# Router logits from rows that are not normalised yet, and a combine with sums and norms fused tile by tile

## The chip, the core and the metric

The kernel is one program on 1 core of one Trainium2 chip. Its time is device microseconds from start to end of one execution; the inputs lie in the chip's memory. The engines are TensorE (PE, matmuls and transposes), VectorE (DVE), ScalarE (ACT), GpSimd (POOL) and SyncE (SP), which issues most of the loads. Each engine runs its own instructions in the order in which the program lists them and waits for the others by semaphores.

## The reference

A first block (four mixers and a dense feed-forward) makes 512 rows of 1024 columns from `x`. Then 16 meta rows are put ahead of them and two layers follow. A layer is a mixer and a mixture of 32 experts, each with a layer norm behind it:

```python
for i in range(2):
    mixed = rglru_mixer(h, ...) if i == 0 else shortconv_mixer(h, ...)
    h = layer_norm(ALPHA * h + mixed, ln_g[i, 0], ln_b[i, 0])
    ffn = hierarchical_moe(h, ...)     # router on h, best group, best two of its eight experts
    h = layer_norm(ALPHA * h + ffn, ln_g[i, 1], ln_b[i, 1])
return h[:, 16:]

# layer_norm
mu = mean(x); var = mean((x - mu) ** 2)
y = (x - mu) * rsqrt(var + 1e-5) * g + b
# router
glog = h @ w_group + b_group           # 4 columns
elog = h @ w_expert + b_expert         # 32 columns
# lru mixer ends in (scan * gelu) @ w_out; short convolution:
zc = causal_conv(cg * v); mixed = (bg * zc) @ w_out
```

Only the last two meta rows matter to what is returned, since the short convolution of layer 1 looks back by two rows.

## The kernel before

The rows are kept as four tiles `xt` of 128 rows, and a fifth, `hm`, of the two meta rows, which lives until the short convolution. Products that need full precision are made in three passes of a split: a rounded half (`zh`, `hhi`, `sh_0h`, made by ACT) and the rest (`zl`, `hlo`, `sh_0l`, made by DVE).

**From the mixer to the router** (`mix_ln`, twice). `token_mm` multiplies the mixer's result by `w_out`, tile by tile and in two halves of 512 columns, into `pz`; the last tile of rows comes last. With `steps` set, `sum_` (L1830) adds `pz` to the row tile as soon as a half is there. `ln_sums` (L1622) squares on ACT, small operations on DVE make the mean (`lnm`) and the scale (`lnrr`), `ln_norm` (L1629) normalises on ACT. `Moe.xpose` transposes the normalised tile on PE (`prt`), DVE and ACT copy it (`rht`, L2061), `Moe.route` multiplies it by the router's weights `wr` (36 columns) and adds the bias row `brt` by one more product (`plg`). `ln_gain` (L1638) applies the norm's gain and bias, on DVE and, for a part of the columns of all but the last tile, on POOL. `Moe.fold` has multiplied the gain into `wr` and the bias into `brt` (PE: `pbr<-wr,par`), so the router works on rows without gain. Behind the last tile `Moe.logits` copies all logits (L2078), and the router's choice begins with `gm` (L2114).

**The experts** (`moe`). 32 experts' weights are streamed by SP through buffers `sr`; PE multiplies sorted rows by them. Each row's two results are kept in memory.

**The combine** (end of `moe`). For each tile the two results `cy` are read back, scaled by the gates `gt`, added to the rows, and normalised. The table `COMBINE` sets in which order the steps of the tiles are written: S sums, N norm, G gain, T transposes for the next mixer; M is a form for the meta rows in layer 0 that uses ACT and POOL. `GPC` says how many columns of a gain are DVE's, the rest are POOL's. In layer 0 the meta rows come first, and T of tiles 2 and 3 is left to the short convolution (`e.left`).

**The short convolution** (`shortconv`) multiplies the transposed rows in two halves of columns `HV`, of 258 and 256, the first with the two meta columns ahead.

Of the kernel before, what the change touches and what calls it, by code (L numbers as in the profile page):

```python
# [8 lines left out]
F32 = mybir.dt.float32  # L9
# [8 lines left out]
P = 128  # L18
S = 512
# [26 lines left out]
ORDER[NP // 2:NP // 2] = range(NST, NST + MORE)  # L46
NB = (NP + MORE + 1) // 2 * 2
CT = 32
GPC = ((640, 448, 640, 384, 448), (832, 832, 512, 320))
COMBINE = ("M4 S0 S1 N0 N1 S2 S4 N4 G0 G1 G4 T0 T1 T4 S3 N2 G2 N3 G3", "S0 S1 N0 S2 N1 S3 N2 G0 G1 N3 G2 G3")  # L50
MOE_W = ("moe_w_gate_2", "moe_w_up_2", "moe_w_down_2")
EPS = 1e-6
LN_EPS = 1e-5
# [1442 lines left out]
def token_mm(e, nk, xx, done, tiles, before_tail=None, tail=8, steps=False):  # L1496

    left = deque()
    st = e.st
    for h in range(2):
        pz = [e.bank(f"pz{t}") for t in range(len(tiles))]

        def part(w, k, i):
            tk = tiles[i]
            e.mm3(pz[i][:tk.stop - tk.start], (xx[0][k][:, tk], xx[1][k][:, tk]), (w[0], w[1]), k == 0, k == nk - 1)

        k = 0
# [8 lines left out]
        if h == 1:  # L1520
            if before_tail:
                before_tail()
            ww = [st.get() for _ in range(tail // 2)]
            for i in range(len(tiles)):
                for j in range(tail):
                    part([x[:, j % 2, :] for x in ww[j // 2]], nk - tail + j, i)
                if steps:
                    new = done(i, 1, pz[i])
                    last = list(left)[-1:]
                    with e.tc.manual_schedule(engines=VA):  # L1530
                        for g in [new] + last + [new] + last:
                            next(g)
                        if len(left) > 1:
                            next(left.popleft(), None)
                    left.append(new)
                    continue
                if len(left) >= 2:
                    left.popleft()()
                left.append(done(i, 1, pz[i]))
    return left  # L1540
# [271 lines left out]
def mix_ln(e, sp, zz, tiles, hs, mo):  # L1812


    e.st.limit = e.mark2 if mo.l else e.mark
    g = e.brow(sp, "ln_g_2", D, off=(mo.l * 2) * D, tag="lng0")
    b = e.brow(sp, "ln_b_2", D, off=(mo.l * 2) * D, tag="lnb0")
    sums = {}
    mo.fold()

    def done(i, h, p_):
        if h:
            return steps(i, p_)
        sum_(i, h, p_)

    def sum_(i, h, p_):
        n = tiles[i].stop - tiles[i].start
        c = slice(h * 512, h * 512 + 512)
        s_ = sums[i, h] = sp.tile([P, 1], F32, name=f"sum{i}{h}")[:n]
        e.V.scalar_tensor_tensor(hs[i][:, c], hs[i][:, c], ALPHA, p_[:n], op0=OP.mult, op1=OP.add, accum_out=s_)  # L1830

    def steps(i, p_):
        sum_(i, 1, p_)
        n = tiles[i].stop - tiles[i].start
        nm, ss = ln_sums(e, sp, hs[i], n, [sums[i, 0], sums[i, 1]], sp.tile([P, D], BF, name="lnj")[:n])
        yield
        ln_norm(e, sp, hs[i], n, nm, ss)
        yield
        ht = mo.xpose(sp, hs[i], n)
        yield  # L1840
        t = i - (len(tiles) - NT)
        t = NT if t < 0 else t
        ln_gain(e, hs[i], n, g, b, 0 if i == len(tiles) - 1 else 448)
        mo.keep(t, hs[i], n)
        yield
        mo.route(ht, t, n)

# [47 lines left out]
def shortconv(e):  # L1895
    tc, I, st, sch = e.tc, e.I, e.st, e.sch
    V, A, G, Q = e.V, e.A, e.G, e.Q
    xt, bank, pc = e.xt, e.bank, e.pc
    TH = 258
    HV = (slice(0, TH), slice(TH, TK))  # L1900
    e.mo = Moe(e, 1, None)
    zp = tc.tile_pool(name="sz", bufs=1, reuse_waits="tile")
    zpool = zp.__enter__()
# [2 lines left out]
    sp = sp_.__enter__()  # L1906

    def put(kind, cg, pr, hv, p_):
        if kind == 0:
            A.copy(cg[:, hv], p_)  # L1910
        else:
            e.mul(pr[:, hv], cg[:, hv], p_)
# [9 lines left out]
    for j in range(0, KT, 2):  # L1922
# [40 lines left out]
class Moe:  # L1963
# [76 lines left out]

        self.e.G.dma_start(self.dh[t * P:t * P + n, :], h)

    def fold(self):

        e = self.e
        pg, pb = [e.pc((n, 2 * D) if self.l else n, 0, KT) for n in ("ln_g_2", "ln_b_2")]
        pt = e.bank("pbr")[0:1, :36]
        for k in range(KT):
            e.mm(pt, pb[:, k:k + 1], self.wr[:, k, :], k == 0, k == KT - 1)
        e.add(self.br, self.br, pt)  # L2050
        e.mul(self.wr, self.wr, pg.unsqueeze(2).to_broadcast([P, KT, 36]))
# [12 lines left out]
    def route(self, ht, t, n):  # L2064

        e = self.e
        if self.pl is None:
            self.pl = e.bank("plg"), (e.bank("plg") if self.nt > NT else None)
        pl = self.pl[0][:, t * 36:(t + 1) * 36] if t < NT else self.pl[1][:n, :36]
        for k in range(KT):  # L2070
            e.mm(pl, ht[:, k, :n], self.wr[:, k, :], k == 0, False)
        e.mm(pl, self.one[:, :n], self.br[0:1, :], False, True)
        if t == NT:
            e.A.copy(self.lg[:n, t, :], pl)

    def logits(self):

        self.done = self.e.A.copy(self.lg[:, :NT, :].rearrange("p t c -> p (t c)"), self.pl[0][:, :NT * 36])  # L2078

    def run(self):  # L2080
        moe(self.e, self)
# [3 lines left out]
def moe(e, mo):  # L2085
# [406 lines left out]
        e.act3 = tc.tile_pool(name="act3", bufs=1, side="right", reuse_waits="tile")  # L2492
        e.open_act(e.act3.__enter__())
    with tc.tile_pool(name=f"cb{l}", bufs=1, reuse_waits="tile") as sp:
        order = [NT, 0, 1, 2, 3] if l == 0 else range(NT)
        ys = {}
        with tc.manual_schedule(engines={mybir.EngineType.SP}):
            for t in order:
                if l == 0 and t == NT - 1:
                    st.stop()  # L2500
                    st.prefetch()
                n = rows_[t][1]
                ys[t] = sp.tile([P, 2, D], F32, name="cy", bufs=4)
                Q.dma_start(ys[t][:n], dy[2 * t * P:2 * (t * P + n), :].rearrange("(t k) c -> t k c", k=2))
        def sums(h, n, t):
            y_ = ys[t][:n]
            stt(h, y_[:, 0, :], gt[:n, t, 0:1], h, OP.mult, OP.add)
            sm = sp.tile([P, 1], F32, name="csum", bufs=4)[:n]
            V.scalar_tensor_tensor(h, y_[:, 1, :], gt[:n, t, 1:2], h, op0=OP.mult, op1=OP.add, accum_out=sm)  # L2509
            return ln_sums(e, sp, h, n, [sm], y_[:, 0, :])  # L2510

        def scaled(h, n, t):

            y_ = ys[t][:n]
            for k in range(2):
                A.activation(y_[:, k, :], y_[:, k, :], AF.Copy, scale=gt[:n, t, k:k + 1])
                G.tensor_tensor(h, h, y_[:, k, :], op=OP.add)
            yield
            sm = sp.tile([P, 1], F32, name="msum")[:n]
            A.activation(y_[:, 0, :], h, AF.Identity, accum_out=sm)  # L2520
            yield ln_sums(e, sp, h, n, [sm], y_[:, 0, :], "m")

        def step(c, t):
            h, n = rows_[t]
            if c == "M":
                ms[t] = scaled(h, n, t)
                next(ms[t])
            elif c == "S":
                ms[t] = next(ms[t]) if t == NT else sums(h, n, t)
            elif c == "N":  # L2530
                ln_norm(e, sp, h, n, *ms[t], "m" if t == NT else "")
            elif c == "G":
                ln_gain(e, h, n, g, b, GPC[l][t])
                if l == 1:
                    Q.dma_start(e.out[0, t * P:(t + 1) * P, :], h)
            else:
                e.tile_to_fm(h, 2 + t * P if t < NT else 0, n)

        ms = {}
        with tc.manual_schedule(engines={mybir.EngineType.DVE, mybir.EngineType.Activation, mybir.EngineType.Pool}):  # L2540
            t = order[0]
# [40 lines left out]
```

## Time and profile before

| | us |
|---|---|
| median of 3 runs | 2554.92 (2554.54 to 2555.36) |
| the profiled execution | 2554.61 |
| its span | 2552.8 |
| PE busy | 2300.2 (90%) |
| DVE busy | 944.4 (37%) |
| ACT busy | 666.8 (26%) |
| POOL busy | 226.5 (9%) |

The span is divided into the first block, the lru mixer (to about 1260), the experts of layer 0 (to about 1757), the combine and the short convolution (to about 2005), the experts of layer 1 and the last combine. Over most of the expert layers the DMA moves 412 to 419 GB/s. The granted clock of PE was 0.964 in the mean; between stretches it takes the levels 0.5 (1.2 GHz) and 1.0 (2.4 GHz).

### The profile page before, as it was taken

The numbers are of one execution on the slowest core, as the hardware profiler recorded it, in microseconds if no ns is written. First come the engines' busy times: TensorE is split into PE (matmuls) and PEld (weight loads), VectorE is DVE, ScalarE is ACT, GpSimd is POOL, SyncE is SP. The second block draws the span as 40 slices with busy tenths as digits, with TensorE's granted clock in tenths as the row PEclk, the third lists the DMA queues.
The fourth block names the chain that finished last, engine by engine and source line by source line (L and its number), as shares of the span: only waits on it lengthen the run. The fifth ranks groups of instructions, "written<-read, shape, count | busy, mean of one in ns | idle before, by whom it ended". The sixth has DMA issues, their size and how long they took to land. (4 is left out here: it accounts for less than half of the span.)

```text
span 2552.8 us, 37528 instructions
## 1 busy us (share of the span) xinstructions
PE 2300.2 (90%) x15343; PEld 1470.3 (58%) x15343; DVE 944.4 (37%) x2162; ACT 666.8 (26%) x1058; POOL 226.5 (9%) x264
## 2 busy tenths in 40 slices
PE   7998999999999999999799899884899798899881
PEld 6886777877888888887632233221798532233220
DVE  4348868765533332565620000003644610000003
ACT  4335432123422322375300000013322210000012
POOL 0023120000100000100200000001200210000002
PEclk9999999999999999999799999997899799999996
DMA  4221221025133242224589999998225599999993
GB/s 142 91 80 43 87 70 63 23 79 187 53 106 92 90 140 91 80 82 147 221 342 418 419 415 416 412 415 313 61 87 227 224 399 418 419 413 414 415 405 122
DMA packets 176434, 556.87 MB, mean 218 GB/s; under 512 B 22248, under 2 KB 104934, under 8 KB 127106
## 3 DMA queue, kind: packets, MB, share of 16 engines
q1 hardware_dynamic: 154308, 523.29, 53.0%
q0 software_dynamic: 12768, 25.31, 2.7%
q10 hardware_dynamic: 9184, 5.84, 0.8%
q8 instruction: 122, 2.00, 0.3%
q14 instruction: 52, 0.43, 0.1%
HBM read 548.02 MB, written 25.21 MB: 225 GB/s over the span
## 5 line engine op out<-in xcount | busy, mean ns | idle before, releaser
L300 PE MATMUL peg<-sr,ext 128*32 128x512 f32 (+1 forms) x4064 | 527.6, 599 | 70.9 <-DMA sr<-in_moe_w_gate_dram 38.7
L300 PEld LDWEIGHTS peg<-sr,ext 128*32 128x32 f32 (+1 forms) x4064 | 142.4, 111 | 410.8 <-issue 276.7
L300 PE MATMUL pey<-sr,eh 128*32 128x512 f32 x1984 | 303.3, 597 | 14.1 <-DMA sr<-in_moe_w_down_dram 11.8
L300 PEld LDWEIGHTS pey<-sr,eh 128*32 128x32 f32 x1984 | 82.0, 110 | 193.5 <-issue 148.6
L227 DVE TENSOR_TENSOR sh_0l<-sr,sh_0h 128x1024 fp32r<-128x1024 f32 x84 | 103.5, 1232 | 163.4 <-ACT sh_0h L225 162.8
L285 DVE TENSOR_TENSOR eh<-eh,peg 128x512 f32<-128x512 f32 x34 | 23.4, 688 | 367.4 <-PE peg L300 367.4
L2321 ACT COPY eys<-pey 128x512 f32<-128x512 f32 x68 | 39.9, 586 | 428.9 <-PE pey L300 428.4
L225 ACT CAST sh_0h<-sr 128x1024 fp32r<-128x1024 f32 x84 | 88.1, 1049 | 238.4 <-PE pf L300 53.2
L2264 DVE COPY ext<-pex 128x512 f32<-128x512 f32 x32 | 22.0, 689 | 311.1 <-PE pex L319 311.1
L227 DVE TENSOR_TENSOR sh_1l<-sr,sh_1h 128x1024 fp32r<-128x1024 f32 (+1 forms) x65 | 77.4, 1191 | 107.0 <-ACT sh_1h L225 106.7
L227 DVE TENSOR_TENSOR sh_2l<-sr,sh_2h 128x1024 fp32r<-128x1024 f32 (+1 forms) x65 | 74.2, 1141 | 94.5 <-ACT sh_2h L225 94.2
L225 ACT CAST sh_1h<-sr 128x1024 fp32r<-128x1024 f32 (+1 forms) x65 | 66.5, 1022 | 147.3 <-PE pf L300 48.5
L225 ACT CAST sh_2h<-sr 128x1024 fp32r<-128x1024 f32 (+1 forms) x65 | 62.9, 967 | 151.8 <-PE pf L300 49.3
L2290 ACT ACTIVATE eh<-peg 128x512 f32<-128x512 f32 x34 | 20.3, 597 | 278.0 <-PE peg L300 278.0
L300 PE MATMUL pl<-hlo,sh_0h 128*128 128x264 f32 (+3 forms) x288 | 87.5, 304 | 2.2 <-DVE hlo L309 2.2
L300 PE MATMUL pl<-hhi,sh_0h 128*128 128x264 f32 (+3 forms) x288 | 87.8, 305 | 0.8 <-ACT hhi L308 0.8
L300 PE MATMUL pl<-hhi,sh_0l 128*128 128x264 f32 (+3 forms) x288 | 87.0, 302 | 0.0
L2322 POOL DMA_INDIRECT dy<-eys,yix x34 | 33.9, 998 | 576.2 <-ACT eys L2321 559.8
L2300 DVE COPY eh<-pex 128x512 f32<-128x512 f32 x34 | 23.3, 691 | 136.0 <-PE pex L319 136.0
L2178 POOL DMA_INDIRECT xg<-dh,tix x34 | 35.4, 1041 | 326.3 <-PE pex L319 244.7
L2264 ACT COPY ext<-pex 128x512 f32<-128x512 f32 x36 | 21.1, 586 | 163.2 <-PE pex L319 118.7
L300 PEld LDWEIGHTS pl<-hlo,sh_0h 128*128 128x128 f32 x288 | 56.2, 195 | 5.0 <-DVE hlo L309 3.2
(747 smaller groups left out, 4898.2 us busy)
## 6 DMA issues: line engine op xcount, KB each, us to landing
sr<-in_moe_w_gate_dram SPq DMA_DIRECT2D x128, 1024.0 KB
sr<-in_moe_w_up_dram SPq DMA_DIRECT2D x122, 1024.0 KB
sr<-in_moe_w_down_dram SPq DMA_DIRECT2D x122, 1024.0 KB
sr<-in_w_in_dram SPq DMA_DIRECT2D x34, 1024.0 KB
sr<-in_sc_w_in_dram SPq DMA_DIRECT2D x12, 1024.0 KB
sr<-in_ffn_w_gate_dram SPq DMA_DIRECT2D x11, 1024.0 KB
sr<-in_ffn_w_up_dram SPq DMA_DIRECT2D x11, 1024.0 KB
sr<-in_ffn_w_down_dram SPq DMA_DIRECT2D x10, 1024.0 KB
```

The source lines that it names most:

```text
L225: self.e.A.copy(hi, r)
L227: v.tensor_tensor(lo, r, f(hi), op=OP.subtract)
L285: V.tensor_tensor(out_, a, b, op=OP.mult)
L300: T.matmul(o, l, r, start=start, stop=stop)
L2178: G.indirect_dma_start(out=xg[i], out_offset=None, in_=dh[:, :], in_offset=bass.IndirectOffsetOnAxis(ap=ti, axis=0), bounds_check=n_tok - ...
L2264: (A.copy if k0 or first else V.tensor_copy)(x_[:, k0:k0 + 4, :].rearrange("p k c -> p (k c)"), pt)
L2290: A.activation(sg, pg, AF.Silu)
L2300: V.tensor_copy(hh.rearrange("p k c -> p (k c)"), pt)
L2321: e.late = A.copy(ys[:, h * 512:(h + 1) * 512], po[h])
L2322: G.indirect_dma_start(out=dy[:, :], out_offset=bass.IndirectOffsetOnAxis(ap=yi, axis=0), in_=ys, in_offset=None, bounds_check=2 * n_tok - ...
```

## The change

The router's logits are made from rows that are not normalised. With raw row `x`, mean `m` and scale `r`, the logits are `r * (x @ w - m * sum(w)) + b`. So transposes and router products follow the sum at once; `fold` also makes the column sums of `wr` and a copy of the bias on all partitions (`rcb`, by products with a tile of ones, `rone`); `scales` keeps each tile's minus mean and scale (`rmr`); and `logits` applies them with four DVE operations to the four tiles and four to the meta rows. `token_mm` calls the steps at other points.

The combine of layer 0 is written tile by tile: S sums, Q square on ACT, A `(x - m) * g`, R scale, B `* r + b`, with the meta rows last and in the same form as the others. The short convolution has the meta columns last, in its second half.

```diff
-GPC = ((640, 448, 640, 384, 448), (832, 832, 512, 320))
-COMBINE = ("M4 S0 S1 N0 N1 S2 S4 N4 G0 G1 G4 T0 T1 T4 S3 N2 G2 N3 G3", "S0 S1 N0 S2 N1 S3 N2 G0 G1 N3 G2 G3")
+GPC = (None, (832, 832, 512, 320))
+COMBINE = ("S0 Q0 A0 R0 B0 S1 Q1 T0 A1 R1 B1 S2 Q2 T1 A2 R2 B2 S3 Q3 A3 R3 B3 S4 Q4 A4 R4 B4", "S0 S1 N0 S2 N1 S3 N2 G0 G1 N3 G2 G3")
...
                     part([x[:, j % 2, :] for x in ww[j // 2]], nk - tail + j, i)
+                    if steps and left and j == tail // 2 - 1:
+                        with e.tc.manual_schedule(engines=VA):
+                            next(left[0])
                 if steps:
-                    new = done(i, 1, pz[i])
-                    last = list(left)[-1:]
+                    left.append(done(i, 1, pz[i]))
                     with e.tc.manual_schedule(engines=VA):
-                        for g in [new] + last + [new] + last:
-                            next(g)
+                        next(left[-1])
                         if len(left) > 1:
                             next(left.popleft(), None)
...
         nm, ss = ln_sums(e, sp, hs[i], n, [sums[i, 0], sums[i, 1]], sp.tile([P, D], BF, name="lnj")[:n])
-        yield
-        ln_norm(e, sp, hs[i], n, nm, ss)
+        r = e.rsq(sp, ss, n, LN_EPS, "lnr")
+        mo.scales(t, n, nm, r)
         yield
         ht = mo.xpose(sp, hs[i], n)
-        yield
+        e.mul(nm, nm, r)
+        e.A.activation(hs[i], hs[i], AF.Identity, scale=r, bias=nm)
         ln_gain(e, hs[i], n, g, b, 0 if i == len(tiles) - 1 else 448)
...
-    TH = 258
-    HV = (slice(0, TH), slice(TH, TK))
+    HV = (slice(0, W0), slice(W0, TK))
...
+    def fold(self, pool):
+        ones, self.cb, self.mr = [pool.tile([P] + sh, F32, name=n) for n, sh in
+                                  (("rone", [P]), ("rcb", [72]), ("rmr", [2, self.nt]))]
+        e.V.memset(ones, 1.0)
...
+        pt = e.bank("pbr")
+        for k in range(KT):
+            e.mm(pt[:, :36], ones, self.wr[:, k, :], k == 0, k == KT - 1)
+        e.mm(pt[:, 36:72], self.one, self.br, True, True)
+        e.V.tensor_copy(self.cb, pt[:, :72])
...
     def logits(self):
-        self.done = self.e.A.copy(self.lg[:, :NT, :].rearrange("p t c -> p (t c)"), self.pl[0][:, :NT * 36])
+        for t0, t1, n, pl in ((0, NT, P, self.pl[0]), (NT, self.nt, 2, self.pl[1])):
+            if t0 < t1:
...
+                e.V.tensor_tensor(lg, row(0), of(0), op=OP.mult)
+                e.add(lg, lg, pl[:n, :(t1 - t0) * 36].rearrange("p (t c) -> p t c", c=36))
+                e.V.tensor_tensor(lg, lg, of(1), op=OP.mult)
+                e.V.tensor_tensor(lg, lg, row(1), op=OP.add)
...
-        order = [NT, 0, 1, 2, 3] if l == 0 else range(NT)
+        order = range(nt)
...
+            elif c == "Q":
+                A.activation(sp.tile([P, D], BF, name="cj", bufs=2)[:n], h, AF.Square, bias=ms[t][0], accum_out=ms[t][1])
+            elif c == "A":
+                stt(ms[t][2], h, ms[t][0], g[:n], OP.add, OP.mult)
+            elif c == "R":
+                ms[t][1] = e.rsq(sp, ms[t][1], n, LN_EPS, "cr")
+            elif c == "B":
+                stt(h, ms[t][2], ms[t][1], b[:n], OP.mult, OP.add)
...
-            e.left = [lambda t=t: step("T", t) for t in (2, 3)]
+            e.left = [lambda t=t: step("T", t) for t in (2, 3, NT)]
```

How this moves instructions: on DVE at the end of the lru mixer of layer 0, `lgx` is the mixer's result, `zl` its rest, `sh_*l` the rests of weights, `hm,sum` the first `sum_`. Before:

```order
L285 TENSOR_TENSOR lgx<-lm_10197,yb 128x514 x2
L227 TENSOR_TENSOR sh_0l<-sr_2_9595,sh_0h 128x1024
L309 TENSOR_TENSOR zl_8967<-lgx,zh_8959 128x514
L309 TENSOR_TENSOR zl_8968<-lgx,zh_8960 128x514
L227 TENSOR_TENSOR sh_2l<-sr_2_9595,sh_2h 128x1024
L227 TENSOR_TENSOR sh_1l<-sr_1_9771,sh_1h 128x1024
L1830 SCALAR_TENSOR_TENSOR hm,sum_10414<-hm,pz_10279 2x512
```

And now:

```order
L285 TENSOR_TENSOR lgx<-lm_10197,yb 128x514 x2
L309 TENSOR_TENSOR zl_8967<-lgx,zh_8959 128x514
L309 TENSOR_TENSOR zl_8968<-lgx,zh_8960 128x514
L2050 MEMSET rone 128x128
L2062 COPY rcb<-pbr 128x72
L227 TENSOR_TENSOR sh_0l<-sr_2_9595,sh_0h 128x1024
L227 TENSOR_TENSOR sh_2l<-sr_2_9595,sh_2h 128x1024
L227 TENSOR_TENSOR sh_1l<-sr_1_9771,sh_1h 128x1024
L1829 SCALAR_TENSOR_TENSOR hm,sum_10429<-hm,pz_10294 2x512
```

The memset of `rone` and the copy of `rcb` have come in behind the last `zl`, and a weight split has moved behind them. On PE at the same place (the products of the gates `pl`, the fold's `pbr`, the first output projection `pz`), now:

```order
L300 MATMUL pl<-lxc,lru_w_a_8969 64x264 x4
L300 MATMUL pl<-lxc,lru_w_i_8972 64x264 x4
L300 MATMUL pbr<-wr,par 1x36 x8
L300 MATMUL pbr<-wr,rone 128x36 x8
L300 MATMUL pbr<-brt,stage_6616 128x36
L300 MATMUL pz_10294<-sh_0h,zh_8953 2x512
```

Before, `pz` followed `pbr<-wr,par` directly; the two groups between are new. On DVE at the last tile of layer 0, from its `sum_` to the router's `gm`, before:

```order
L1830 SCALAR_TENSOR_TENSOR xt,sum_10740<-xt,pz_10452 128x512
L2026 COPY row_11869<-ident 2x128
L294 TENSOR_SCALAR lnm<-sum_10446,sum_10740 128x1
L2061 COPY rht<-prt 128x512
...
L2061 COPY rht<-prt 128x512
L1638 TENSOR_TENSOR xt<-xt,lng_10264 128x1024
L1638 TENSOR_TENSOR xt<-xt,lnb_10266 128x1024
L2114 TENSOR_REDUCE gm<-lg 128x5
```

And now:

```order
L1829 SCALAR_TENSOR_TENSOR xt,sum_10798<-xt,pz_10467 128x512
L2077 COPY rht<-prt 128x512
L294 TENSOR_SCALAR lnm<-sum_10461,sum_10798 128x1
...
L1637 TENSOR_TENSOR xt<-xt,lng_10264 128x1024
L1637 TENSOR_TENSOR xt<-xt,lnb_10266 128x1024
L2098 TENSOR_TENSOR lg<-rcb,rmr 128x144
L288 TENSOR_TENSOR lg<-lg,plg 128x144
L2100 TENSOR_TENSOR lg<-lg,rmr 128x144
L2101 TENSOR_TENSOR lg<-lg,rcb 128x144
...
L2137 TENSOR_REDUCE gm<-lg 128x5
```

The copy of the last tile's transposes stands ahead of its mean, and the logits' operations stand behind both gains.

## Rows read from the trace of the kernel before

**Rows 1.** The page's part 1: busy us (share) xinstructions of two engines.
```profile
PE 2300.2 (90%) x15343; PEld 1470.3 (58%) x15343; DVE 944.4 (37%) x2162; ACT 666.8 (26%) x1058; POOL 226.5 (9%) x264
```

**Rows 2.** Timeline of SP, 1249 to 1284: start us, us, engine line operation.
```profile
1249.82 0.33 SPq L201 DMA_DIRECT2D sh_0l<-in_moe_w_down_dram  x1
1283.11 0.33 SPq L204 DMA_DIRECT2D sr<-in_moe_w_down_dram  x1
```

**Rows 3.** Windows: stretch, busy PE, PEld, DVE, ACT, POOL, clock, DMA share, GB/s.
```profile
1270.00:1275.00 5.00, 0.00 (x0) 0.00 (x0) 5.00 (x9) 0.00 (x0) 2.34 (x2) 0.50 0.10 23
```

**Rows 4.** Timeline of PE at the fold, layer 0.
```profile
1183.40 0.68 PE L300 MATMUL pbr<-wr,par 128*1 128x36 f32 x16
1184.01 0.39 PE L300 MATMUL pz<-sh_0h,zh 128*2 128x512 f32 x1
```

**Rows 5.** Timeline of ACT and DVE at the mixer's end, layer 0.
```profile
1195.13 1.23 ACT L308 CAST zh<-lgx 128x514 fp32r<-128x514 f32 x2 [2.92 <-DVE lgx L285]
...
1196.75 1.29 DVE L309 TENSOR_TENSOR zl<-lgx,zh 128x514 fp32r<-128x514 f32 x2
```

**Rows 6.** Timeline of PE at the fold, layer 1.
```profile
1944.69 0.51 PE L300 MATMUL pz<-sh_0h,zh 128*128 128x512 f32 x1
```

**Rows 7.** Timeline of DVE at the mixer's end, layer 1.
```profile
1946.41 0.67 DVE L309 TENSOR_TENSOR zl<-szc,zh 128x512 fp32r<-128x512 f32 x1
```

**Rows 8.** Timeline of PE at the last tiles, layer 0.
```profile
1237.69 1.87 PE L300 MATMUL plg<-wr,rht 128*128 128x36 f32 x16
1239.49 0.41 PE L300 MATMUL plg<-brt,stage 1*128 1x36 f32 x2
...
1245.53 1.03 PE L319 MATMUL prt<-ident,xt 128*128 128x128 f32 x8
...
1252.91 3.63 PE L300 MATMUL plg<-wr,rht 128*128 128x36 f32 x16
```

**Rows 9.** Timeline of DVE at the last tile, layer 0.
```profile
1245.72 0.69 DVE L1830 SCALAR_TENSOR_TENSOR xt<-xt,pz 128x512 f32<-128x512 f32 x1 [3.32 <-PE pz L300]
...
1253.08 1.23 DVE L1638 TENSOR_TENSOR xt<-xt,lng 128x1024 f32<-128x1024 f32 x1 [0.23 <-PE prt L319]
...
1257.51 0.18 DVE L2114 TENSOR_REDUCE gm<-lg 128x5 f32<-128x20 f32 x1 [1.94 <-ACT lg L2078]
...
1259.09 0.33 DVE L285 TENSOR_TENSOR sel<-lg,ge 128x160 f32<-128x160 f32 x1
```

**Rows 10.** Timeline of ACT at the last tile, layer 0.
```profile
1246.70 1.15 ACT L1622 ACTIVATE lnj<-xt,lnm 128x1024 bf16<-128x1024 f32 x1 [4.48 <-DVE lnm L294]
...
1249.68 1.24 ACT L1629 ACTIVATE xt<-xt,lnm,lnrr 128x1024 f32<-128x1024 f32 x1 [1.07 <-DVE lnm L285]
```

**Rows 11.** Timeline of DVE at the last tile, layer 1.
```profile
1992.98 0.69 DVE L1830 SCALAR_TENSOR_TENSOR xt<-xt,pz 128x512 f32<-128x512 f32 x1 [3.22 <-PE pz L300]
...
2004.75 0.17 DVE L2114 TENSOR_REDUCE gm<-lg 128x4 f32<-128x16 f32 x1 [1.96 <-ACT lg L2078]
```

**Rows 12.** Timeline of DVE and POOL in the combine, layer 0.
```profile
1769.48 1.28 DVE L297 SCALAR_TENSOR_TENSOR xt<-cy,gt,xt 128x1024 f32<-128x1024 f32 x1
...
1770.62 5.63 POOL L2517 TENSOR_TENSOR hm<-hm,cy 2x1024 f32<-2x1024 f32 x2 [11.91 <-ACT cy L2516]
...
1770.80 3.25 DVE L2509 SCALAR_TENSOR_TENSOR xt<-cy,gt,xt 128x1024 f32<-128x1024 f32 x1
```

**Rows 13.** Timeline of PE between combine and short convolution.
```profile
1795.02 1.94 PE L319 MATMUL pth<-ident,xt 128*128 128x128 f32 x8 [38.25 <-DVE xt L1638]
...
1802.05 0.58 PE L300 MATMUL pl<-hlo,sh_0h 128*128 128x258 f32 x1 [0.24 <-DVE hlo L309]
...
1815.28 1.03 PE L319 MATMUL pth<-ident,xt 128*128 128x128 f32 x8
...
1818.14 0.38 PE L300 MATMUL pl<-hhi,sh_0h 128*128 128x256 f32 x1
```

**Rows 14.** Windows, as in rows 3: the clock in the first half.
```profile
1806.50:1807.00 0.50, 0.50 (x4) 0.50 (x4) 0.43 (x3) 0.00 (x0) 0.00 (x0) 0.70 0.40 60
```

More of the change, by code (lines that the diff above doesn't have):

```diff
@@ L1526, in token_mm @@
                     part([x[:, j % 2, :] for x in ww[j // 2]], nk - tail + j, i)
+                    if steps and left and j == tail // 2 - 1:
+                        with e.tc.manual_schedule(engines=VA):
+                            next(left[0])
                 if steps:
-                    new = done(i, 1, pz[i])
-                    last = list(left)[-1:]
+                    left.append(done(i, 1, pz[i]))
                     with e.tc.manual_schedule(engines=VA):
-                        for g in [new] + last + [new] + last:
-                            next(g)
+                        next(left[-1])
                         if len(left) > 1:
                             next(left.popleft(), None)
-                    left.append(new)
                     continue
@@ L1818, in mix_ln @@
     sums = {}
-    mo.fold()
+    mo.fold(sp)
     def done(i, h, p_):
@@ L1834, in steps @@
         n = tiles[i].stop - tiles[i].start
+        t = i - (len(tiles) - NT)
+        t = NT if t < 0 else t
         nm, ss = ln_sums(e, sp, hs[i], n, [sums[i, 0], sums[i, 1]], sp.tile([P, D], BF, name="lnj")[:n])
-        yield
-        ln_norm(e, sp, hs[i], n, nm, ss)
+        r = e.rsq(sp, ss, n, LN_EPS, "lnr")
+        mo.scales(t, n, nm, r)
         yield
         ht = mo.xpose(sp, hs[i], n)
-        yield
-        t = i - (len(tiles) - NT)
-        t = NT if t < 0 else t
+        e.mul(nm, nm, r)
+        e.A.activation(hs[i], hs[i], AF.Identity, scale=r, bias=nm)
         ln_gain(e, hs[i], n, g, b, 0 if i == len(tiles) - 1 else 448)
@@ L1908, in put @@
     def put(kind, cg, pr, hv, p_):
[L1909 to L1912, printed above, removed]
+        for c0, n in ((hv.start, W0),) + (((S, 2),) if hv.stop > S else ()):
+            to = slice(2 + c0, 2 + c0 + n) if c0 < S else slice(0, 2)
+            if kind == 0:
+                A.copy(cg[:, to], p_[:, c0 - hv.start:c0 - hv.start + n])
+            else:
+                e.mul(pr[:, to], cg[:, to], p_[:, c0 - hv.start:c0 - hv.start + n])
     def finish(j, pr, pb):
@@ L1950, in shortconv @@
             pb = bank("pl")
-            for _ in e.chunk_mm(pb, st.get(), slice(2, TK)):
+            for _ in e.chunk_mm(pb, st.get(), slice(0, S)):
                 pass
@@ L2041, in keep, with scales @@
         self.e.G.dma_start(self.dh[t * P:t * P + n, :], h)
-    def fold(self):
+    def fold(self, pool):
         e = self.e
+        ones, self.cb, self.mr = [pool.tile([P] + sh, F32, name=n) for n, sh in
+                                  (("rone", [P]), ("rcb", [72]), ("rmr", [2, self.nt]))]
+        e.V.memset(ones, 1.0)
         pg, pb = [e.pc((n, 2 * D) if self.l else n, 0, KT) for n in ("ln_g_2", "ln_b_2")]
-        pt = e.bank("pbr")[0:1, :36]
+        pt = e.bank("pbr")
         for k in range(KT):
-            e.mm(pt, pb[:, k:k + 1], self.wr[:, k, :], k == 0, k == KT - 1)
-        e.add(self.br, self.br, pt)
+            e.mm(pt[0:1, :36], pb[:, k:k + 1], self.wr[:, k, :], k == 0, k == KT - 1)
+        e.add(self.br, self.br, pt[0:1, :36])
         e.mul(self.wr, self.wr, pg.unsqueeze(2).to_broadcast([P, KT, 36]))
+        pt = e.bank("pbr")
+        for k in range(KT):
+            e.mm(pt[:, :36], ones, self.wr[:, k, :], k == 0, k == KT - 1)
+        e.mm(pt[:, 36:72], self.one, self.br, True, True)
+        e.V.tensor_copy(self.cb, pt[:, :72])
+    def scales(self, t, n, nm, r):
+        self.e.V.tensor_copy(self.mr[:n, 0, t:t + 1], nm)
+        self.e.V.tensor_copy(self.mr[:n, 1, t:t + 1], r)
     def xpose(self, pool, h, n):
@@ L2070, in route @@
         for k in range(KT):
[L2071 to L2074, printed above, removed]
+            e.mm(pl, ht[:, k, :n], self.wr[:, k, :], k == 0, k == KT - 1)
     def logits(self):
-        self.done = self.e.A.copy(self.lg[:, :NT, :].rearrange("p t c -> p (t c)"), self.pl[0][:, :NT * 36])
+        e = self.e
+        for t0, t1, n, pl in ((0, NT, P, self.pl[0]), (NT, self.nt, 2, self.pl[1])):
+            if t0 < t1:
+                sh = [n, t1 - t0, 36]
+                lg = self.lg[:n, t0:t1, :]
+                of = lambda k: self.mr[:n, k, t0:t1].unsqueeze(2).to_broadcast(sh)
+                row = lambda k: self.cb[:n, k * 36:(k + 1) * 36].unsqueeze(1).to_broadcast(sh)
+                e.V.tensor_tensor(lg, row(0), of(0), op=OP.mult)
+                e.add(lg, lg, pl[:n, :(t1 - t0) * 36].rearrange("p (t c) -> p t c", c=36))
+                e.V.tensor_tensor(lg, lg, of(1), op=OP.mult)
+                e.V.tensor_tensor(lg, lg, row(1), op=OP.add)
     def run(self):
@@ L2504, in moe @@
                 Q.dma_start(ys[t][:n], dy[2 * t * P:2 * (t * P + n), :].rearrange("(t k) c -> t k c", k=2))
[L2505 to L2521, printed above, removed]
@@ L2523, in step @@
         def step(c, t):
             h, n = rows_[t]
[L2525 to L2529, printed above, removed]
+            if c == "S":
+                y_ = ys[t][:n]
+                stt(h, y_[:, 0, :], gt[:n, t, 0:1], h, OP.mult, OP.add)
+                sm = sp.tile([P, 1], F32, name="csum", bufs=4)[:n]
+                V.scalar_tensor_tensor(h, y_[:, 1, :], gt[:n, t, 1:2], h, op0=OP.mult, op1=OP.add, accum_out=sm)
+                if l == 1:
+                    ms[t] = ln_sums(e, sp, h, n, [sm], y_[:, 0, :])
+                else:
+                    nm = sp.tile([P, 1], F32, name="cnm", bufs=4)[:n]
+                    ts(nm, sm, -1.0 / D)
+                    ms[t] = [nm, sp.tile([P, 1], F32, name="css", bufs=4)[:n], sp.tile([P, D], F32, name="ct", bufs=2)[:n]]
+            elif c == "Q":
[6 more added lines that the diff above has]
+                stt(h, ms[t][2], ms[t][1], b[:n], OP.mult, OP.add)
@@ L2530, in step @@
             elif c == "N":
-                ln_norm(e, sp, h, n, *ms[t], "m" if t == NT else "")
+                ln_norm(e, sp, h, n, *ms[t])
             elif c == "G":
                 ln_gain(e, h, n, g, b, GPC[l][t])
-                if l == 1:
-                    Q.dma_start(e.out[0, t * P:(t + 1) * P, :], h)
+                Q.dma_start(e.out[0, t * P:(t + 1) * P, :], h)
             else:
-                e.tile_to_fm(h, 2 + t * P if t < NT else 0, n)
+                e.tile_to_fm(h, t * P, n)
```

## The prediction

> **What bounds the kernel now.** I read the page's busy shares first, then the stretches around the three places that the change touches. TensorE is busy for 90% of the span and no other engine for half of that [rows 1], so whatever stops PE counts unless something else was going to be late anyway. The only thing that could be is the weight stream of the experts. It isn't late at the start of an expert layer: SP issued one load at 1249.82 and the next at 1283.11 [rows 2], and between, the DMA moved 23 GB/s [rows 3]. All weight buffers are full and wait for the first expert to free one. A microsecond that the router comes later therefore moves the whole expert layer by a microsecond, and no stream absorbs it. The chain that ended last is not what I argue from; it lies in the final combine, which keeps its steps.
>
> The sum is made against the profiled execution: 2554.61 us, its span 2552.8 and 1.8 around it; the runs have a median of 2554.92, 0.3 above. What a measurement of this kernel can tell from no change is about 0.2%, 5.1 us.
>
> **The fold, layer 0.** Before, PE ends the eight narrow products `pbr<-wr,par` and goes straight on at 1184.01 with the output projection `pz` [rows 4]. Now eight more products `pbr<-wr,rone` of 128x36 and one for the bias stand between them on PE. They need `rone`, a tile that DVE fills with ones. On DVE that memset stands behind `lgx` and both `zl` splits of the recurrence. Before, the last two splits ran from 1196.75 to 1198.04, behind one weight split of about 1 us that now stands behind them; what they take in, ACT's `zh`, is there at 1195.13 + 1.23 = 1196.36 [rows 5]. So the second split ends at 1196.4 + 0.7 = 1197.1, and with 0.2 for the memset (an estimate by the 0.18 of the shortest DVE row, [rows 9]) I take 1197.3. So PE, which had 13 us of ready `pz` work, has nothing to run from 1184.0 to 1197.3. Then come 16 passes, which take 1.87 at the full clock (1237.69) and 3.63 at the half one (1252.91) [rows 8]; I take 3.6, and 0.5 for the bias: `pz` starts at 1201.4 instead of 1184.01, **+17.4**. All of this is on the path, since `pz`, the sums and the router follow on PE. What hid the recurrence's DVE tail before was `pz` itself, and that cover is gone. After such a stop the granted clock is 0.5: in the stretch after the 38 us stop of the combine PE works at it from 1800.6 and it rises at 1806.75 [rows 14] (its 0.70 is a mean of the two levels). The fold's own passes use some of that time, so the start of `pz` loses between 0.5 and 2.7; I take 1.0. **Layer 0 fold: +18.4.**
>
> The Trainium skill, "TensorE: Matmul & The Clock Gate" (section "Step-by-step: what each phase is for"), says that only weight loads are pulled ahead and that matmuls keep program order. By that rule the blocked `pbr` holds all of `pz` and the sum is +18.4; if PE could pass it, the term would shrink to the passes, 2.2. The trace agrees with the rule: at 1802.05 PE stood idle for 0.24 on `hlo` while products with `hhi` stood ready behind it [rows 13].
>
> **The fold, layer 1.** The same order, but here the wait is short: PE would stop at 1944.69 [rows 6], the last `zl` ends at 1947.08 [rows 7], the memset at 1947.3; the passes at full clock take 1.87 + 0.34, so `pz` starts at 1949.5: **+4.8**. If 2.6 us of waiting lets the clock fall, the passes double and the first `pz` too: +8.5.
>
> **The last tile, layer 0.** The logits now multiply the raw rows, so transposes and router products no longer wait for a norm. Behind the norm come four DVE operations per group of tiles: mean, sum, scale, bias. Take T as the time at which the last `pz` matmul gives way to the narrow products, 1245.53 [rows 8]. Before, the products of tile 2's transpose and tile 1's logits came after T; now they come in among the last `pz`. That is 0.9 and 1.8 (1.03 and 1.87 less the overlap of their ends), less 0.5 for two bias products that are gone (0.41 for a whole tile) [rows 8], so T' = T + 2.2. From T' on, PE does tile 2's logits (1.80) and then the last transposes (about 0.9), which DVE copies at T' + 2.4 to 3.1. The copy stands ahead of `lnm` on DVE, so the square on ACT starts at T' + 3.35; before it started at T + 1.17 [rows 10]. From the square to the end of the norm is 1249.68 + 1.24 - 1246.70 = 4.22, and two small copies of mean and scale add 0.35: T' + 7.9. Then the two gains of 128x1024 at 1.23 each [rows 9], since all of the last tile's columns are DVE's: T' + 10.45. Only behind these stand the logits' four operations on 144 columns, for which the nearest row is 0.33 at 160 columns plus some 0.03 between [rows 9], and four on 2x36 at about 0.13 (`gm`'s 0.18 less the overlap): 1.95. The first router operation `gm` comes at T' + 12.35. Before it came at 1257.51, T + 11.98. So **+2.6**; from both sides 0 (if DVE has its earlier work done sooner than I think) to +5.
>
> **The last tile, layer 1.** No meta rows, so no 2x36 operations: T' is later by 0.9 + 1.8 - 0.4 = 2.3, `gm` at T' + 11.83 against 2004.75 - 1992.98 + 0.19 = 11.96 [rows 11]: **+2.2**.
>
> **The combine of layer 0 and its handover.** PE had been idle for 38.25 us when it began to transpose at 1795.02 and `hlo` of the first half came at 1802.05 [rows 13]. Two things go. POOL took part in it (5.63 for two additions on the meta rows), and DVE's product beside it took 3.25 where the same shape had taken 1.28 just before [rows 12]; POOL has nothing to do there now. And the norm is fused into products over whole rows: per tile two sums 2.6, mean 0.2, one fused 1.3, scale 0.9 (five operations near the 0.18 of `gm`), one fused 1.3, together 6.3, with ACT only squaring. From 1769.48 two tiles are done at 1782.1, and `hlo` follows 5.1 behind the second tile's transposes as before: 1787.2, or **-14.9**.
>
> But the meta rows are last now. The first half takes 13.2 as before (until the next transposes at 1815.28 [rows 13]) and ends at 1800.4; the second half begins with the meta rows' columns among its 258, so it waits for the fifth tile. DVE has five times 6.3 of norms and some 7 of splits between them to do and gets there at 1808.1 (an operation on 2 partitions of 1024 costs what one on 128 does, its length being the same). Its fifth matmul can go at 1810.7 and the first at about 1809, where before it was 1818.14 [rows 13]: 8.2 to 9.1 sooner. PE stands from 1802.5 to 1809, and a stop costs the clock again; by the 1800.6 to 1806.75 of [rows 14] that is some 2.2. **-6.0**; ends: -3 (clock, and DVE some 3 us later) and -14.9 (the meta wait hidden). I take the value nearest to DVE's own sum of rows. The two extra column operations per piece in the short convolution lie beside full matmul columns and cost nothing; if that cover were gone they would be 16 operations of about 0.18 [rows 9], 2.9 us.
>
> The DVE rate has a rule of its own in the Trainium skill, "SBUF — State Buffer" (section "🔬 SBUF: two separate sides"): DVE and GpSimd share a port pair, and one locks the other out. The trace agrees with its 3.25 against 1.28 [rows 12]. Without the rule, taking 3.25 as DVE's own price, the fused combine would give back most of its gain, and the sum would be some 10 us worse.
>
> **Sum:** 18.4 + 4.8 + 2.6 + 2.2 - 6.0 = +22.0; 2554.61 + 22.0 = **2576.6 us**.
>
> **Rivals.**
> *The clock falls at every stop.* Layer 0's `pz` loses 2.7 instead of 1.0, layer 1's fold 8.5 instead of 4.8, the combine gains 3 instead of 6: 22.0 + 1.7 + 3.7 + 3 = 30.4, **2585.0**. For it: each stop of PE that I looked at ended at 0.5. Against it: the wait in layer 1 is 2.6 us. The same page of the Trainium skill on TensorE (section "Why this matters for your kernels") says that gaps between bursts bring the slow clock back, which is this rival's case.
> *The combine gains more.* If DVE reaches the meta rows some 6 us earlier, -12 instead of -6: **2570.6**. For it: the sum of DVE's rows is mine, and ACT may take splits. Against: everything of it is in sequence on one engine.
> *The other side: the fold doesn't stop PE.* This is one mechanism: if ones are in place before PE asks, because the memset isn't held behind `zl`, each fold costs its passes alone, 2.2, and with the full -14.9 at the combine the sum is 4.4 + 4.8 - 14.9 = -5.7, **2548.9**. It decides as soon as both folds cost under 10.1 together with the full combine gain. Against it: the DVE order and the 0.24 of [rows 13].
> *The logits come early, as the change says.* Were they ahead of the gains, `gm` would be some 4 us earlier in each layer: **2568.6**. Against it: in DVE's order they stand behind both gains.
>
> **Chances.** Forecast 50% (2572 to 2581 by its own bounds), clock 20%, combine 19%, early logits 4%, no stop 7%. Of the last a part lies within 0.2%. So faster 0.06, same 0.04, slower 0.90. The range 2565 to 2587 leaves out the no-stop case, and the outer ends of clock and combine.
>
> **What would show it.** In the profile after: PE idle from 1184 to about 1197 with `rone` or DVE as what ended it, and `pz` at 1201; about 2.6 idle at 1945; `gm` behind both gains in each layer; products of 1.28 throughout the combine, the first half's `hlo` near 1787 + 21 (the shift until there), and PE idle again between the halves with a granted clock of 0.5. The prediction is wrong if `pz` starts within 4 us of its old place, or if PE has no gap between the halves.

## The result, and the profile after

The changed kernel takes 2577.01 us (median of 4 runs, 2575.29 to 2578.55), the kernel before 2554.73. The ratio is 1.0087, 95% interval 1.0073 to 1.0102: slower by 22.3 us, where 22.0 was forecast. The profiled execution is the slowest of the four, 2578.55, 23.94 above that of before.

The page's first part of the kernel after: every engine has about the work that it had [rows 1], PE 2.5 us more, so the 23.9 are waiting and a slower clock.

```profile
PE 2302.7 (89%) x15361; PEld 1473.3 (57%) x15361; DVE 950.9 (37%) x2202; ACT 657.1 (26%) x1054; POOL 211.4 (8%) x252
```

The timeline of PE at the fold of layer 0, after (start us, us, line, operation; in brackets the idle time before it and what ended it), which answers to [rows 4]:

```profile
1185.63 0.68 PE L300 MATMUL pbr<-wr,par 128*1 128x36 f32 x16
1199.59 3.60 PE L300 MATMUL pbr<-wr,rone 128*128 128x36 f32 x16 [13.27 <-DVE rone L2050]
1203.12 0.64 PE L300 MATMUL pbr<-brt,stage 1*128 1x36 f32 x2
1203.68 0.59 PE L300 MATMUL pz<-sh_0h,zh 128*2 128x512 f32 x1
```

And of DVE beside it, which answers to [rows 5]:

```profile
1198.00 1.30 DVE L309 TENSOR_TENSOR zl<-lgx,zh 128x514 fp32r<-128x514 f32 x2
1199.28 0.17 DVE L2050 MEMSET rone<- 128x128 f32 x1
```

PE stands for 13.27 us and the profile names the memset, which began as the second split ended. From `pbr` to `pz` it is 18.05 instead of 0.61. The windows of the same stretch (stretch, busy PE, PEld, DVE, ACT, POOL, clock, DMA share, GB/s) show the clock fall during the stop and stay at 0.50 until past 1208:

```profile
1190.00:1199.00 9.00, 0.00 (x0) 0.00 (x0) 6.54 (x9) 4.25 (x6) 0.00 (x0) 0.58 0.03 4
1199.00:1204.00 5.00, 4.41 (x19) 4.07 (x20) 0.65 (x3) 0.00 (x0) 0.00 (x0) 0.50 0.90 294
1204.00:1208.00 4.00, 4.00 (x11) 2.23 (x10) 0.03 (x1) 0.00 (x0) 0.00 (x0) 0.50 0.99 403
1208.00:1212.00 4.00, 4.00 (x18) 3.24 (x17) 0.00 (x0) 0.00 (x0) 0.00 (x0) 0.94 1.01 427
```

PE at the fold of layer 1, after, against [rows 6] (where before `pbr` had begun at 1944.08); the second fence has windows of the stop and of what follows:

```profile
1959.19 0.68 PE L300 MATMUL pbr<-wr,par 128*1 128x36 f32 x16
1962.49 3.30 PE L300 MATMUL pbr<-wr,rone 128*128 128x36 f32 x16 [2.61 <-DVE rone L2050]
...
1966.28 0.80 PE L300 MATMUL pz<-sh_0h,zh 128*128 128x512 f32 x1
```

```profile
1960.00:1962.40 2.40, 0.00 (x0) 0.00 (x0) 2.34 (x5) 0.69 (x2) 0.00 (x0) 1.00 0.85 249
1962.00:1966.00 4.00, 3.51 (x18) 3.47 (x18) 0.34 (x2) 0.00 (x0) 0.00 (x0) 0.60 1.02 419
1966.00:1969.00 3.00, 3.00 (x8) 2.36 (x8) 0.23 (x1) 0.00 (x0) 0.00 (x0) 0.50 1.00 340
```

Here the stop is 2.61 us. The clock was 1.00 during it and fell as the passes began (the 0.60 is a mean of the two levels): they took 3.30 and not 1.87, and the first `pz` stood at 0.50 too.

DVE at the last tile of layer 0, after, against [rows 9]:

```profile
1270.87 0.68 DVE L1829 SCALAR_TENSOR_TENSOR xt<-xt,pz 128x512 f32<-128x512 f32 x1
...
1271.81 0.69 DVE L2077 COPY rht<-prt 128x512 f32<-128x512 f32 x1 [0.26 <-PE prt L319]
1272.42 0.20 DVE L294 TENSOR_SCALAR lnm<-sum,sum 128x1 f32<-128x1 f32 x1
...
1276.75 1.22 DVE L1637 TENSOR_TENSOR xt<-xt,lng 128x1024 f32<-128x1024 f32 x1 [1.31 <-ACT xt L1842]
1278.01 1.23 DVE L1637 TENSOR_TENSOR xt<-xt,lnb 128x1024 f32<-128x1024 f32 x1
1279.15 0.30 DVE L2098 TENSOR_TENSOR lg<-rcb,rmr 128x144 f32<-128x144 f32 x1
...
1281.38 0.18 DVE L2137 TENSOR_REDUCE gm<-lg 128x5 f32<-128x20 f32 x1
```

The mean waits behind the copy of the transposes, and the logits behind the norm on ACT (1.31) and both gains. PE beside it:

```profile
1269.44 1.87 PE L300 MATMUL plg<-wr,rht 128*128 128x36 f32 x16
...
1272.56 1.98 PE L300 MATMUL plg<-wr,rht 128*128 128x36 f32 x16 [0.29 <-DVE rht L2077]
```

The last router product took 1.98 from 1272.56, so its result lay ready for 4.6 us before the logits began.

PE from the combine to the short convolution, after, against [rows 13], with the last expert's products ahead of it:

```profile
1776.28 3.63 PE L300 MATMUL pey<-sr,eh 128*32 128x512 f32 x24 [1.06 <-SPq L2499]
...
1799.11 1.97 PE L319 MATMUL pth<-ident,xt 128*128 128x128 f32 x8 [19.20 <-DVE xt L297]
1808.17 1.97 PE L319 MATMUL pth<-ident,xt 128*128 128x128 f32 x8 [7.10 <-DVE xt L297]
1812.63 0.58 PE L300 MATMUL pl<-hhi,sh_0h 128*128 128x256 f32 x1 [2.49 <-ACT hhi L308]
...
1832.10 0.98 PE L319 MATMUL pth<-ident,hm 2*128 2x2 f32 x8 [4.63 <-DVE hm L297]
1833.02 0.58 PE L300 MATMUL pl<-hhi,sh_0h 128*128 128x258 f32 x1
```

The two halves have a stop of 4.63 between them, which the meta rows end. The first operations of the combine take what they took before POOL's additions [rows 12], all through:

```profile
1793.82 1.28 DVE L2535 SCALAR_TENSOR_TENSOR xt<-cy,gt,xt 128x1024 f32<-128x1024 f32 x1
...
1803.54 1.29 DVE L309 TENSOR_TENSOR hlo<-pth,hhi 128x512 fp32r<-128x512 f32 x2 [1.78 <-ACT hhi L308]
```

Two more lines of the trace of before are needed to read shifts: the last expert's products of layer 0, and `pbr` of layer 1.

```profile
1753.14 3.63 PE L300 MATMUL pey<-sr,eh 128*32 128x512 f32 x24 [1.08 <-SPq L2476]
...
1944.08 0.68 PE L300 MATMUL pbr<-wr,par 128*1 128x36 f32 x16
```

And `gm` of layer 1, after:

```profile
2029.42 0.17 DVE L2137 TENSOR_REDUCE gm<-lg 128x4 f32<-128x16 f32 x1
```

The same place read against the trace of before gives a shift. It was +2.2 at `pbr` of layer 0, ahead of anything changed, +19.7 at the first `pz`, +23.9 at `gm`, +23.1 at the last expert's products, +15.1 at `pbr` of layer 1, +21.6 at its `pz`, +24.7 at its `gm`, +24.0 at the last products of layer 1, where it stayed. In other kernels below, whose program is the same up to `pbr`, it began between 1182.95 and 1185.12, so most of the 2.2 is the spread of executions.

### The profile page after: what moved, and what is told of

Same layout as the page of the kernel before. It is cut to its first block, busy times and chain, and to the rows that moved or that the text cites. A ratio compares the mean times of both kernels' runs of the same rounds, so it can differ in the third digit from the quotient of the medians.

```text
span 2576.7 us, 37584 instructions
## 1 busy us (share of the span) xinstructions
PE 2302.7 (89%) x15361; PEld 1473.3 (57%) x15361; DVE 950.9 (37%) x2202; ACT 657.1 (26%) x1054; POOL 211.4 (8%) x252
## 5 line engine op out<-in xcount | busy, mean ns | idle before, releaser
L300 PEld LDWEIGHTS pl<-hhi,sh_0h 128*128 128x128 f32 x288 | 56.5, 196 | 6.4 <-ACT hhi L308 4.1
```

The source lines that it names most:

```text
L300: T.matmul(o, l, r, start=start, stop=stop)
```

## The experiments

Ratios are to the kernel before, with 95% intervals.

**Sums late.** The products with ones go behind the last router product.

```diff
+        self.ones = ones
+    def sums(self):
         pt = e.bank("pbr")
         for k in range(KT):
-            e.mm(pt[:, :36], ones, self.wr[:, k, :], k == 0, k == KT - 1)
+            e.mm(pt[:, :36], self.ones, self.wr[:, k, :], k == 0, k == KT - 1)
...
+        mo.sums()
         mo.logits()
```

> The changed kernel with the products of the ones tile (pbr<-wr,rone) and the copy of rcb behind the last router product instead of ahead of the output projection. Theory (PE in order, stopped by rone): both stops go, pz starts again as in the kernel before; the 17.4 of layer 0, about 1 of slow clock and the 6.5 of layer 1 come back: 2577.0 - 24.9 = 2552 us; the 16 passes lie beside the norm of the last tile and cost nothing. Rival (PE would soon have stopped on the late zl anyway, the memset is only the first to show it): less than half comes back, 2565 or more.

Measured: 2550.04 us, 0.9981 (0.9971 to 0.9990), 27.0 less than the changed kernel. In its trace `pz` follows `pbr` by 0.61 in both layers, as before the change; in layer 0:

```profile
1183.36 0.68 PE L300 MATMUL pbr<-wr,par 128*1 128x36 f32 x16
1183.97 0.39 PE L300 MATMUL pz<-sh_0h,zh 128*2 128x512 f32 x1
```

Both folds with their stops and passes (17.4 and 6.5 in the trace) and the slow clock behind them were the loss. From the start of the first `pz` to that of the last it is 63.35 and 50.09 here, and 65.52 and 51.62 in the changed kernel, so the slow clock costs 2.2 and 1.5 there. The late `zl` cost PE nothing by itself.

**Ones early.** The tile of ones is filled when the mixer begins.

```diff
-        e.V.memset(ones, 1.0)
+        ones = self.ones
...
+        e.mo.ones = state["zp"].tile([P, P], F32, name="rone")
+        V.memset(e.mo.ones, 1.0)
```

> The changed kernel with the ones tile filled when the layer's mixer begins, in a pool of its own; the products stay ahead of the output projection. Theory (the wait for the memset costs, the products little): each fold costs its 16 passes and the wait for wr, 2.5 to 2.7: 2577.0 - 15.7 - 4.0 = 2557 us. Rival (the products and the clock that falls with them cost, not the wait): 2570 or more.

Measured: 2556.03 us, 1.0005 (0.9996 to 1.0015), 21.0 less than the changed kernel. PE at its folds, and the window behind the second:

```profile
1182.92 0.68 PE L300 MATMUL pbr<-wr,par 128*1 128x36 f32 x16
1184.34 1.95 PE L300 MATMUL pbr<-wr,rone 128*128 128x36 f32 x16 [0.73 <-ACT ltg L1766]
...
1186.55 0.40 PE L300 MATMUL pz<-sh_0h,zh 128*2 128x512 f32 x1
...
1939.95 1.95 PE L300 MATMUL pbr<-wr,rone 128*128 128x36 f32 x16 [0.73 <-DVE wr L285]
...
1942.28 0.80 PE L300 MATMUL pz<-sh_0h,zh 128*128 128x512 f32 x1
```

```profile
1942.00:1945.00 3.00, 3.00 (x8) 2.36 (x9) 0.23 (x1) 0.00 (x0) 0.00 (x0) 0.50 1.02 419
```

The same instructions at the same place, without the wait for ones, cost 3.0 in layer 0 and 3.1 in layer 1 (3.63 and 3.74 from `pbr` to `pz`, less 0.61), with the passes at the full clock. Behind them the clock stayed at 1.00 in layer 0; in layer 1 it fell to 0.50, which cost the start of `pz` another 1.4 (51.53 from the first `pz` to the last, 50.09 with the sums late). So of the 27.0, 21 are the wait and the clock that went with it, and 6 the products on the path with what they bring: 0.7 in each layer is the wait for `wr` (the profile names it in layer 1; in layer 0 it names ACT, but `wr` ended at 1184.19, just ahead of the passes).

**The combine alone**: the kernel before with the table, the steps and the short convolution of the change.

```diff
-COMBINE = ("M4 S0 S1 N0 N1 S2 S4 N4 G0 G1 G4 T0 T1 T4 S3 N2 G2 N3 G3", ...
+COMBINE = ("S0 Q0 A0 R0 B0 S1 Q1 T0 A1 R1 B1 S2 Q2 T1 A2 R2 B2 S3 Q3 A3 R3 B3 S4 Q4 A4 R4 B4", ...
```

> The kernel before with the new combine of layer 0 and the new columns of the short convolution alone. Theory: the traces' shift between the last expert's product and the fold of layer 1, -8.0, is the combine's own: 2554.7 - 8.0 = 2547 us. Rival (the gain is given back by weights that come later or was a gift of the shift by 23 us): 2553 to 2555.

Measured: 2546.55 us, 0.9971 (0.9959 to 0.9982): 8.0 less. The gain is the combine's own.

**The router alone**: the kernel before with the fold, steps and logits of the change.

```diff
-    mo.fold()
+    mo.fold(sp)
...
-        e.mm(pl, self.one[:, :n], self.br[0:1, :], False, True)
```

> The kernel before with the new fold, steps and logits alone, the old combine. Theory: the two parts add up, 2577.0 + 8.0 = 2585 us. Rival (the parts share a loss, for instance the clock): 2580 or less.

Measured: 2582.65 us, 1.0109 (1.0092 to 1.0126): 28.1 more, between the 2585 of the theory and the 2580 of the rival. With the combine's -8.0 that makes 20.0, where both together cost 22.3; the difference is within the intervals of the two. PE at its fold of layer 1:

```profile
1968.56 1.95 PE L300 MATMUL pbr<-wr,rone 128*128 128x36 f32 x16 [2.61 <-DVE rone L2048]
...
1970.77 0.64 PE L300 MATMUL pz<-sh_0h,zh 128*128 128x512 f32 x1
```

```profile
1971.00:1974.00 3.00, 3.00 (x8) 2.31 (x8) 0.11 (x1) 0.00 (x0) 0.00 (x0) 0.50 1.00 339
```

The same stop of 2.61 as in the changed kernel, but here the passes still ran at the full clock, and the clock fell only behind them.

**Logits first.** The sums late, though on PE ahead of the last router product; the norm of every tile in two products on DVE; and, of the logits, the first operation ahead of the last tile's second product and the others right behind it.

```diff
+        ct = sp.tile([P, D], F32, name="lnc")[:n]
+        e.stt(ct, hs[i], nm, g[:n], OP.add, OP.mult)
...
-        e.mul(nm, nm, r)
-        e.A.activation(hs[i], hs[i], AF.Identity, scale=r, bias=nm)
-        ln_gain(e, hs[i], n, g, b, 0 if i == len(tiles) - 1 else 448)
+        last = lambda: e.stt(hs[i], ct, r, b[:n], OP.mult, OP.add)
+        if i == len(tiles) - 1:
+            mo.logits(last)
```

> The changed kernel with the sums late and, in both layers, the norm fused as in the combine (product with the gain beside ACT's square, scale and bias in one more), all of it on DVE, and the logits of the last tile ahead of everything but one such product. Theory (the logits lost their gain because they stood behind both gains and behind the copy of the last transposes): the first router operation comes about 8.8 behind the last output projection instead of 12.1, in both layers: 2550.0 - 6.7 = 2543 us. Rival (the router products on PE end last, the order on DVE matters little): 2548 or more.

Measured: 2543.27 us, 0.9955 (0.9939 to 0.9972), 6.8 less than with the sums late alone (6.6 by the ratios). How this divides among the three parts of the edit was not measured. DVE and PE at its last tile:

```profile
1248.82 0.69 DVE L1830 SCALAR_TENSOR_TENSOR xt<-xt,pz 128x512 f32<-128x512 f32 x1 [1.36 <-PE pz L300]
...
1253.74 0.31 DVE L2112 TENSOR_TENSOR lg<-rcb,rmr 128x144 f32<-128x144 f32 x1
1253.96 1.28 DVE L297 SCALAR_TENSOR_TENSOR xt<-lnc,lnrr,lnb 128x1024 f32<-128x1024 f32 x1
1255.78 0.30 DVE L288 TENSOR_TENSOR lg<-lg,plg 128x144 f32<-128x144 f32 x1 [0.54 <-PE plg L300]
...
1257.55 0.17 DVE L2153 TENSOR_REDUCE gm<-lg 128x5 f32<-128x20 f32 x1
```

```profile
1253.36 2.38 PE L300 MATMUL plg<-wr,rht 128*128 128x36 f32 x16
```

From the sum to `gm` it is 8.73, after the change 10.51. The second logits operation now waits for PE (0.54): the router products end last, with the passes of the sums (from 1251.22) just ahead of them on PE.

**Order in the combine.** T0 behind B1, T1 behind S2, on top of it.

```diff
-... S1 Q1 T0 A1 R1 B1 S2 Q2 T1 A2 R2 B2 ...
+... S1 Q1 A1 R1 B1 T0 S2 T1 Q2 A2 R2 B2 ...
```

> As e5_logits_first, with the transposes of tiles 0 and 1 written later in the combine (T0 behind B1, T1 behind S2), so that DVE does not wait for ACT's halves. Theory (DVE's work in a row sets when the halves start; it waits 1.78 twice): first half 3 earlier, meta rows 3.5 earlier, 3 to 3.5 less than e5. Rival (the second half hangs on the meta rows and the slow clock behind its stop, which gets no shorter): under 1 less.

Measured: 2540.24 us, 0.9942 (0.9925 to 0.9958), 3.0 less than logits first, but the intervals of the two overlap. With fold early, which follows, it is the fastest kernel, 36.8 below the changed one and, by the ratio, 14.8 below the one before. PE in its handover:

```profile
1773.41 1.97 PE L319 MATMUL pth<-ident,xt 128*128 128x128 f32 x8 [19.20 <-DVE xt L297]
1779.88 1.97 PE L319 MATMUL pth<-ident,xt 128*128 128x128 f32 x8 [4.51 <-DVE xt L297]
...
1804.08 0.98 PE L319 MATMUL pth<-ident,hm 2*128 2x2 f32 x8 [4.63 <-DVE hm L297]
```

The second transposes come 6.5 behind the first and not 9.1. The stop ahead of the meta rows is 4.63 as before, but 2.8 earlier (1804.08 against 1806.84 in the trace of logits first). Of this 0.6 was there at the last expert's products, so the stage's own part is 2.2, and 1.5 at `pbr` of layer 1 (178.10 from the last expert's last product, against 179.60). DVE's two waits of 1.78 are gone, and one of 1.59 for ACT has come in behind the meta rows' sums (1798.79). So the direction is the theory's, but its 3 to 3.5 is not shown.

**Fold early.** The fold of layer 0 with its sums ahead of the last group of gates.

```diff
+            if g == KT // GR - 1:
+                e.mo.fold(state["zp"])
+                e.mo.sums()
```

> As e6_combine_order, with the whole fold of layer 0 ahead of the last group of gates of the recurrence, where PE is idle for 5.5 afterwards. Theory (fold costs only where PE has no wait to hide it): its passes leave the path, 2.4 less than e6. Rival (they were hidden already behind the last tile's norm): no change.

Measured: 2540.16 us, 0.9940 (0.9924 to 0.9957): no change that the intervals show. In the traces, the last `pz` of layer 0 to `gm` is 7.99 instead of 9.01, so about 1 is gained there and what is left is too small for these runs. It is inconclusive on the rest.

**Meta rows on DVE.** The kernel before without POOL's additions in the combine.

```diff
-COMBINE = ("M4 S0 S1 N0 ...
+COMBINE = ("S0 S1 N0 ...
-                ms[t] = next(ms[t]) if t == NT else sums(h, n, t)
+                ms[t] = sums(h, n, t)
```

> The kernel before with the meta rows' two additions on DVE like those of the other tiles (no POOL additions beside them), all else as before. Theory (the 8.0 of the combine come from fusing norm and gain on one engine): about 2 of POOL's hold on DVE less, two DVE operations of 1.3 more, 2553 to 2555 us. Rival (they come from taking POOL's additions away): 2550 or less.

Measured: 2552.26 us, 0.9989 (0.9979 to 0.9998), 2.8 less than before, with 0.5 to 5.4 in the interval. It lies just outside the theory's 2553 to 2555, and above the rival's 2550. In the trace the stretch from the last expert's last product to `pbr` of layer 1 is 185.66 instead of 187.91, so 2 to 3 of the combine's 8.0 go with POOL's additions. The other 5 are what is left, not a measurement of their own; 1.0 of them lies in the short convolution.

## Why the prediction was right, point by point

**The fold of layer 0, +18.4.** Right in mechanism and size. From `pbr` to `pz` the trace has 17.4 more, as forecast, and sums late and ones early tell the wait from the products.

**The clock at its start and the last tile, layer 0, +1.0 and +2.6.** From the first `pz` to `gm` it is 77.70 instead of 73.50: +4.2 for the forecast 3.6. The clock stayed low to about 1208.3, 4.6 behind `pz`'s start, and cost 2.2, where 1.0 was taken. The narrow products among the last `pz` cost 2.1 (63.35 from the first `pz` to the last with the sums late, 61.29 before), as forecast with 2.2. From the last `pz` to `gm` it is 12.18, before 12.21, where 0.4 more was forecast: the early products bought nothing there. That the logits would stand behind both gains is shown by the rows, and logits first removes it (9.17).

**No cover by the weight stream.** Right: the shift was 23.9 at `gm` and 23.1 at the last products of the experts.

**The combine, -6.0.** It gave -8.0, in the trace and alone. The second half began at 1833.02 - 23.14 = 1809.9, against the forecast 1809, and the clock cost 1.3 there: the half takes 13.23 instead of 11.92 (to 1846.25; before 1818.14 to 1830.06), where 2.2 was assumed. The rest is in the short convolution behind it, costed at nothing: from there to its last 512-column stage the trace has 101.70 instead of 102.70. The first half came later than the forecast 1787: its `hlo` products began at 1813.65 - 23.14 = 1790.5. Between the first two tiles DVE waited 1.78 for ACT's halves and made two splits in 1.3, which the forecast counts only further on; the second tile was done at 1785.0 instead of 1782.1. The late first half cost nothing by itself, since PE then stopped for 4.63 ahead of the meta rows, but DVE's waits are on its way to these as well, as order in the combine shows. The meta rows' products of 2x1024 took 1.27, as those of 128x1024 did (1.27 to 1.29), which the forecast relied on.

**The fold of layer 1, +4.8.** +6.5. This is a mis-sized term. The wait was the forecast's (2.61 for 2.6), but I let the clock fall only in the rival, and it fell as the passes began. In router alone, where it fell behind the passes, the same fold cost 5.50 - 0.61 = 4.9.

**The last tile, layer 1, +2.2.** +3.1 (63.14 from `pz` to `gm` instead of 60.06). Of this 1.5 is the slow clock at the start of `pz`, which the sum put at nothing, and 1.6 the last tile.

The terms in the trace are 17.4, 4.2, -0.7, -8.0, 6.5, 3.1 and -0.7, sum 21.8. With the 2.2 ahead of the fold that makes the 24.0 of the profiled execution; the runs have 22.3. That the sum came out so close is luck. The slow clock behind the two folds cost 2.2 + 1.6 + 1.5 = 5.3 beyond what the wait and the forecast passes took, and the sum had 1.0 for it. Against this error of 4.3 stand 2.0 more from the combine, 1.2 less for the two last tiles, and the -0.7 of each expert layer, for which the forecast had no term.

**The rivals.** The clock falling at every stop was right for both folds and the second half, and for the folds near its prices: 2.2 for 2.7 in layer 0, and 6.5 + 1.5 = 8.0 for 8.5 in layer 1. Its 2585 was missed because it gave the combine only 3. The combine gained more, by 2 and not by 6. The other side is excluded by the 13.27 on the row. That the router gets its logits early is excluded by the rows, and shown possible by logits first.

## What to carry to other kernels

An operand that is trivial to make, such as a tile of ones, can come late all the same, and ahead of a long run of products it then holds all of them. Why the memset came so late is not shown: `fold` writes it first, yet it ran 12.8 us behind the product for `wr` (1186.46). Its tile comes from a pool that opens when the recurrence's closes, so the memory is the likely reason; but ones early changes the pool and the place together. When an operation is moved early so that later work can start, follow it to its last consumer: here the products were early and the four small operations that need them were last in line. A part of a change that loses can hide one that gains, so time the parts apart: here the combine was worth 8.0 us, and with the two stops out, the norms fused, the logits ahead and the combine's order changed, the whole is worth 14.8.

## What was not expected of the hardware

- The length of a stop of PE did not settle whether the work behind it ran slowly. At the fold of layer 1, behind dense work, a stop of 2.61 us was followed by slow passes in the changed kernel (3.30 for 16 passes that take 1.87) and by passes at the full clock in router alone (1.95), with the clock at 0.50 only behind them; a stop of 0.73 in ones early had the same 1.95 and then the same 0.50. In layer 0 of ones early a stop of 0.73 left the clock at 1.00. What decides it was not tested.
- In the short convolution the 48 products of 512 columns took 11.13 to 11.15 where their operand begins at column 0, and 11.23 where it began at column 2 (start to next start); the 24 of 256 columns took 2.80 to 2.85 from column 0 and 2.87 to 2.88 from column 258. That is 1.0 us over the stage. Nothing else was varied to show that the start of the operand is the cause.
